# Lower priority for the additions of the shared products, and new scheduler clocks for the FFN, in a one-core hybrid layer

## The chip, the cores and the metric

The kernel runs on one core of a Trainium2 chip, in one launch. The metric is device microseconds of that core, median over runs. Of the core's engines, TensorE (PE) does the matrix products, VectorE (DVE) and ScalarE (ACT) do the elementwise work, and SyncE (SP) issues almost all of the DMAs.

## The reference

One layer on 256 rows of width 2048, all in float32: RMS norm, one wide input projection, three mixers (mLSTM, attention with forget gates, a conformer convolution), an output projection with a residual, and an FFN. The change touches the FFN alone, which is over half of the time:

```python
x = x + jnp.concatenate([y_m, y_a, y_c], axis=-1) @ w_out
h2 = rmsnorm(x, norm_ffn)
x = x + jnp.square(jax.nn.relu(h2 @ w_up)) @ w_down     # w_up 2048x8192, w_down 8192x2048
...
return rmsnorm(x, final_norm)
```

## The kernel before

**Splits.** To keep float32 accuracy, every operand of a big product is split into a rounded part `hi` and a remainder `lo`, and three products (hi·hi, hi·lo, lo·hi) are accumulated. The weights are split on the fly. One DMA brings a *unit* of 1 MB (4 chunks of 128 rows x 512 columns) into a tile `raw`, of which there are four (`NRAW`). A unit is used in two *steps* of two chunks each. For a step ACT writes `hi` (L424, or L396 in the steps described below), DVE writes `lo` = `raw` - `hi` (L443, or L399), and PE then does the step's matmuls (L57). There are five `hi` and five `lo` tiles (`NHL`), given out in the order in which the instructions are issued; a tile is free again when PE has finished the step that used it. The splits of a step are put up when PE has finished the step five earlier.

**The FFN** goes over the hidden width in four quarters, q = 0 to 3. In a quarter, four blocks of `w_up` make `hid` (16 steps and more of plain matmuls); then two *pairs* of column blocks of `w_down` (p = 0 and p = 1, each 2 x 512 columns) are multiplied, four row groups per pair. A plain step of `w_down` is 12 matmuls of 128x512. In row group 1 of a pair the 2x2 block product is done with seven products instead of eight: seven steps of 6 matmuls, in the order p3, p1, p2, p5, p7, p6, p4 (`SEVEN`). p5, p7, p6 and p4 multiply differences of weight pieces; DVE makes each difference in place in the `raw` tile (L383, "the sum" below) before it is split. In q = 3 the second pair is plain. So there are seven such blocks of seven steps.

**The shared products.** p1, p5, p6 and p7 go to PSUM banks of their own (`extra`). `add_up` collects them: in q = 0 ACT copies them into `acc` (first pair) or into a tile named `fnb` (second pair), in q = 1 to 3 DVE adds them to it (L1218). After the last quarter of a pair (q = 3 for the first, q = 2 for the second) four steps `g` of two DVE instructions each combine the four collected products and add them to the residual `x2t` (L1232 to L1245).

**The order** on ACT, DVE, PE and SP is made when the program is built, by a list scheduler with a clock per engine. Each task has an engine, a cost in us, predecessors and a priority (lower goes first). For each engine `best` takes, among the tasks that are ready at the engine's clock, the one with the lowest priority, then the oldest. PE's clock is advanced by a fixed time per step. The result is one fixed sequence per engine; on the chip an engine takes its sequence strictly in that order and waits where an operand isn't there. A split has priority -1, an addition of a shared product -2 and a step `g` -1.5, so both go ahead of splits that are ready at the same time.

Of the kernel before, what the change touches and what calls it, by code (L numbers as in the profile page):

```python
# [6 lines left out]
F32 = mybir.dt.float32  # L7
# [26 lines left out]
def trunk(ctx: ExitStack, tc, x, norm_mix, w_in, b_in, mlstm_conv_w, mlstm_conv_b,  # L34
# [3 lines left out]
    x, w_in, w_out, w_up, w_down, out = x[0], w_in[0], w_out[0], w_up[0], w_down[0], out[0]  # L38
# [15 lines left out]
    act, dve, pe, pool_e = nc.scalar, nc.vector, nc.tensor, nc.gpsimd  # L54
# [5 lines left out]
    clock = dict(act=0.0, dve=0.0, pool=0.0, pe=0.0, ctl=0.0)  # L60
# [32 lines left out]
    def t_act(cost, fn, *a, **kw):  # L93
        return task("act", cost, fn, *a, **kw)

    def t_dve(cost, fn, *a, **kw):
        return task("dve", cost, fn, *a, **kw)
# [87 lines left out]
    def ca(n, ps=False):  # L185
        return 0.11 + 0.00083 * n + (0.05 if ps else 0.0)

    def cd(n):
        return 0.13 + 0.00105 * n
# [47 lines left out]
    for name, lst in rows.items():  # L237
        rowp[name] = sbt(pl("early"), [P, P], "row" + name)
        colt[name] = sbt(base, [P, P], "col" + name)
        r = 0  # L240
# [80 lines left out]
    hl = {}  # L321
# [3 lines left out]
    loaded = {}  # L325
# [28 lines left out]
    halves = {}  # L354
# [5 lines left out]
    steps = []  # L360
    sums = {}
# [9 lines left out]
    def piece(u, h):  # L371
        return raws[u][0][:, 2 * h:2 * h + 2, :]

    def sum_task(i):

        s = steps[i]
        e, p = s["e"], s["p"]
        o, l, r = {"p5": ((e, 0), (e - 1, 0), (e, 0)),
                   "p7": ((e - 1, 0), (e - 1, 1), (e - 1, 0)),
                   "p6": ((e - 1, 1), (e - 1, 1), (e, 0)),  # L380
                   "p4": ((e, 1), (e, 1), (e - 1, 1))}[p]
        after = [halves[i - {"p5": 2, "p7": 3, "p6": 5, "p4": 4}[p]]] + [sums[k] for k in (i - 1, i - 2) if k in sums]
        sums[i] = t_dve(cd(1024), lambda: dve.tensor_sub(piece(*o), piece(*l), piece(*r)),  # L383
                        after + [loaded[e - 1], loaded[e]], prio=-1)
        return sums[i]

    def split_seven(i, deps):
        s = steps[i]
        u, h = s["u"], s["h"]
        if s["p"] in ("p5", "p7", "p6", "p4"):  # L390
            deps = deps + [sum_task(i)]

        def hi():
            t = sbt(base, [P, 2, 512], "hi", F32R, bufs=NHL)
            hl[i] = [t, sbt(base, [P, 2, 512], "lo", F32R, bufs=NHL)]
            act.activation(t, piece(u, h), AF.Copy)  # L396

        a = his[i] = t_act(ca(1024), hi, deps + [loaded.setdefault(u, Task("none", 0.0, None)), his[i - 1]], prio=-1)
        halves[i] = t_dve(cd(1024), lambda: dve.tensor_sub(hl[i][1], piece(u, h), hl[i][0].bitcast(F32)),  # L399
                          [a], prio=-1)  # L400
        if s["p"] == "p4":
            e = s["e"]
            f1 = [sums[i], halves[i - 1], halves[i - 2]]
            f2 = [halves[i], halves[i - 3]]
            c = t_ctl(lambda: load(e - 1 + NRAW, max(t.fin for t in f1)), f1)
            t_ctl(lambda: load(e + NRAW, max(t.fin for t in f2)), f2 + [c])

    his = {}

    def split_tasks(i, deps):  # L410

        if i >= len(steps):
            return
        if steps[i]["p"]:
            split_seven(i, deps)
            return
        u, h = steps[i]["u"], steps[i]["h"]
        d = units[u]
        n = len(d["ks"]) // 2

        def hi():
            t = sbt(base, [P, n, d["w"]], "hi", F32R, bufs=NHL)
            hl[i] = [t, sbt(base, [P, n, d["w"]], "lo", F32R, bufs=NHL)]
            act.activation(t, raws[u][0][:, h * n:(h + 1) * n, :], AF.Copy)  # L424

        deps = deps + [loaded.setdefault(u, Task("none", 0.0, None))]
        prio = -1 if i >= NHL else -2.005 + 0.02 * i
        a = his[i] = t_act(ca(1024), hi, deps + [his.get(i - 1)], prio=prio)
        last = [a]
        if d["g"]:  # L430
            c, m = (2 * NH, 0) if d["gside"] == "left" else (NF, 2 * NH)
            o = 0 if d["gside"] == "left" else d["w"]
            kr = slice(d["ks"][h * n], d["ks"][h * n] + n)
            wh, wl = wg[:, kr, m:m + c], wg[:, kr, NG + m:NG + m + c]
            ga = t_act(ca(n * c), lambda: act.activation(wh, raws[u][1][:, h * n:(h + 1) * n, o:o + c], AF.Copy),
                       deps, prio=-0.5)
            gd = t_dve(cd(n * c), lambda: dve.tensor_sub(wl, raws[u][1][:, h * n:(h + 1) * n, o:o + c],
                                                         wh.bitcast(F32)), [ga], prio=-0.5)
            gate_parts.append(gd)
            last.append(gd)  # L440

        def lo():
            dve.tensor_sub(hl[i][1], raws[u][0][:, h * n:(h + 1) * n, :], hl[i][0].bitcast(F32))  # L443

        b = t_dve(cd(1024), lo, [a], prio=prio)
        halves[i] = b
        if h == 1:
            if d["g"]:
                last.append(halves[i - 1])
            frees = [b, halves[i - 1]] + last + gate_parts  # L450
            t_ctl(lambda: load(u + NRAW, max(t.fin for t in frees)), frees)
# [109 lines left out]
    for j in range(2):  # L561
        d = []
        stats.append(d)
        for h in range(4):
            a = xs_stat[j][:, h:h + 1]
# [8 lines left out]
    for j in range(2):  # L574
# [9 lines left out]
        for h in range(4):  # L584
            o = xt[j][:, cut(h)]
            if h % 2:
                scaled[j, h] = t_act(0.6, lambda o=o, rs=rs: act.activation(o, o, AF.Copy, scale=rs), [d] + stats[1],
                                     prio=-2.9 + 0.2 * h)
            else:
                scaled[j, h] = t_dve(0.45, lambda o=o, rs=rs: dve.tensor_scalar(o, o, rs, None, op0=OP.mult), [d] + stats[1],  # L590
                                     prio=-2.9 + 0.2 * h)
# [9 lines left out]
    for c2 in range(KC // 2):  # L601
        b = mx_buf()
        ts = []
# [146 lines left out]
    for j in range(2):  # L750
        b = mx_buf()
# [454 lines left out]
    def add_up(p, q, o, fin):  # L1206

        ts = []
        for m, x in enumerate(("p1", "p5", "p6", "p7")):
            def f(m=m, x=x):  # L1210
                if (p, 0) not in acc:
                    acc[p, 0] = sbt(pl("late"), [P, 4, 512], "acc0") if p == 0 else \
                        sbt(pl("late"), [P, D], "fnb").rearrange("p (m n) -> p m n", m=4)
                t = acc[p, 0][:, m, :]
                if q == 0:
                    act.activation(t, o["extra"][x].t, AF.Copy)
                else:
                    dve.tensor_add(t, t, o["extra"][x].t)  # L1218

            deps = [o["done"][x], late_open] + ts[-1:]  # L1220
            if q == 0:
                ts.append(t_act(ca(512, True), f, deps, prio=-2, uses=[o["extra"][x]]))
            else:
                ts.append(t_dve(cd(512), f, deps, prio=-2, uses=[o["extra"][x]]))
        if not fin:
            return []

        def g(i):
            a1, a5, a6, a7 = (acc[p, 0][:, m, :] for m in range(4))

            def out(j, c, t):
                dve.scalar_tensor_tensor(x2[0][:, j, cut(c)], t, rs2[:, j:j + 1], x2[0][:, j, cut(c)],  # L1232
                                         op0=OP.mult, op1=OP.add)

            if i == 0:
                dve.tensor_add(a6, a6, a1)
                out(0, 2 * p, a1)
            elif i == 1:
                dve.tensor_add(a7, a7, a6)
                out(1, 2 * p, a7)  # L1240
            elif i == 2:
                dve.tensor_add(a6, a6, a5)
                out(0, 2 * p + 1, a6)
            else:
                dve.tensor_add(a5, a5, a7)  # L1245
                out(1, 2 * p + 1, a5)

        gs = [ts[-1]]
        for i in range(4):
            gs.append(t_dve(2 * cd(512), lambda i=i: g(i), [gs[-1], rs_t], prio=-1.5))  # L1250
        return gs[1:]

    def x2_ap(j, sl):
# [116 lines left out]

    NU = len(units)
    NS = len(steps)
    items = [(i, (0, 1)) for i in range(NS - 4)]
    for j in range(2):
        items += [(i, (j,)) for i in range(NS - 4, NS)]
# [7 lines left out]
    for i, toks in items:  # L1383
        u, half = steps[i]["u"], steps[i]["h"]
        d = units[u]
        if steps[i]["p"]:
            p, o = steps[i]["p"], steps[i]["o"]
            new = [o["extra"][p]] if p in o["extra"] else []
            need = [halves[i], chunk["sums%d" % o["q"]]] + [chunk[d["b"].key, k % KC] for k in d["ks"]]
            force(lambda: all(t.fin is not None for t in need) and room(new) is not None)  # L1390
            start = max([clock["pe"], room(new)] + [t.fin + LAT for t in need])
            take(new)
            for x_ in new:
                x_.t = bank(o["tag"])
            seven_matmuls(i)
            clock["pe"] = start + 1.3
            if new:
                o["done"][p].fin = clock["pe"]
            split_tasks(i + NHL, [done_at(clock["pe"])])
            extras()  # L1400
            continue
# [22 lines left out]
        if "force_log" in globals():  # L1424
            globals()["force_log"].append((i, clock["pe"], start))
        matmuls(i, toks)
        clock["pe"] = start + (2.6 if len(toks) == 2 else 1.3)
        if d["last"] and half == 1:
            for f in (toks if b.kind == "A" else range(b.n)):
                b.done[f].fin = clock["pe"]  # L1430
# [37 lines left out]
```

## Time and profile before

| | |
|---|---|
| median of 3 runs | 1162.3 us (1162.22, 1162.30, 1165.46) |
| profiled execution: its time, its span | 1167.01 us, 1164.9 us |
| mean granted clock of PE over the span | 0.988 |
| PE, DVE, ACT busy | 1135.5, 804.3, 602.3 us |
| share of PE in the chain that ended last | 95% |

The profile is one execution; the span runs from its first to its last instruction, and the time adds what lies around it (2.1 us). A granted clock of 1.00 is 2.4 GHz, 0.50 is 1.2 GHz; a value between is a stretch that has both. Matmuls overlap in the trace, so PE's pace is read from the starts of two rows.

### The profile page before, as it was taken

What the parts mean: (1) busy time and instruction counts of PE and PEld (TensorE: products, weight loads), DVE (VectorE), ACT (ScalarE), POOL (GpSimd) and SP (SyncE); (2) the same over time, 40 slices, a digit from 0 to 9 for tenths busy, and PEclk for the clock granted to TensorE, in tenths of its full rate; (3) what the DMA queues carried; (4) which work ended last, traced back from release to release, by engine and by line L of the source; (5) the groups of instructions that cost most, each with busy time, mean ns of one, the idle gap of its engine ahead of it and who ended that gap; (6) DMA issues with size and microseconds to landing.
All of it is one profiled execution on the core that took longest, in us unless ns stands there. A gap on an engine that the chain in (4) does not pass through costs nothing.

```text
span 1164.9 us, 14898 instructions
## 1 busy us (share of the span) xinstructions
PE 1135.5 (97%) x5838; PEld 962.3 (83%) x5838; DVE 804.3 (69%) x1083; ACT 602.3 (52%) x840; POOL 17.6 (2%) x40
## 2 busy tenths in 40 slices
PE   8999999999999999999999999999999989999796
PEld 6888888888888888888888887888887878888585
DVE  6679988886665565668765668675658685667663
ACT  6454366777775454445444454444445343544353
POOL 1000000000000000000000000000000000000000
PEclk8999999999999999999999999999999999999899
DMA  8756654557555555555485554476563666653642
GB/s 299 239 181 190 203 155 145 171 155 235 164 179 182 181 181 181 181 187 184 139 285 181 181 187 156 164 253 185 164 216 127 212 224 209 181 181 109 217 145 73
DMA packets 127694, 214.93 MB, mean 185 GB/s; under 512 B 3676, under 2 KB 44936, under 8 KB 127240
## 3 DMA queue, kind: packets, MB, share of 16 engines
q1 hardware_dynamic: 127016, 212.92, 56.3%
q10 hardware_dynamic: 608, 1.06, 0.3%
q8 instruction: 46, 0.75, 0.3%
q14 instruction: 24, 0.20, 0.0%
HBM read 211.87 MB, written 2.10 MB: 184 GB/s over the span
## 4 chain that ended last, share of the span: by engine, by line
PE 95%; DVE 2%; DMA 1%; issue 1%; ACT 0%; POOL 0%; POOLq 0%; ACTq 0%; DVEq 0%
PE mm L57 65%; PE mx L57 29%; DMA x<-in_x_dram 1%; DVE lo L399 0%; DVE x2t L1232 0%; DVE lo L443 0%; PE mx L1162 0%; DMA rowp<-in_norm_mix_dram 0%; DVE acc L1218 0%; PE mx L925 0%; POOL st L294 0%; PE mx L610 0%; ACT x2t L1362 0%; PE mx L958 0%; DVE fnb L1218 0%
## 5 line engine op out<-in xcount | busy, mean ns | idle before, releaser
L443 DVE TENSOR_TENSOR lo<-raw,hi 128x1024 fp32r<-128x1024 f32 x364 | 442.5, 1224 | 288.4 <-ACT hi L424 287.0
L424 ACT ACTIVATE hi<-raw 128x1024 fp32r<-128x1024 f32 x364 | 384.2, 1061 | 426.9 <-PE mm L57 282.1
L57 PE MATMUL mm<-x,hi 128*128 128x512 f32 x640 | 227.8, 400 | 0.0
L57 PE MATMUL mm<-h,hi 128*128 128x512 f32 x512 | 181.5, 399 | 0.0
L57 PE MATMUL mx<-h,hi 128*128 128x512 f32 x512 | 181.2, 399 | 0.0
L57 PE MATMUL mm<-x,lo 128*128 128x256 f32 x640 | 179.5, 280 | 0.0
L57 PE MATMUL mm<-hi,hid 128*128 128x512 f32 x556 | 174.6, 391 | 0.4 <-ACT hi L396 0.4
L57 PEld LDWEIGHTS mm<-x,hi 128*128 128x128 f32 x640 | 120.2, 188 | 28.8 <-ACT tmp L522 0.4
L57 PE MATMUL mm<-h,lo 128*128 128x256 f32 x512 | 143.8, 281 | 0.0
L57 PE MATMUL mx<-h,lo 128*128 128x256 f32 x512 | 143.8, 281 | 0.0
L57 PEld LDWEIGHTS mm<-hi,hid 128*128 128x128 f32 x556 | 105.2, 189 | 22.7 <-ACT hi L396 0.8
L57 PEld LDWEIGHTS mm<-x,lo 128*128 128x128 f32 x640 | 120.9, 189 | 0.1
L57 PEld LDWEIGHTS mm<-h,hi 128*128 128x128 f32 x512 | 96.2, 188 | 24.0 <-DVE x2t L1150 0.2
L57 PEld LDWEIGHTS mx<-h,hi 128*128 128x128 f32 x512 | 96.2, 188 | 23.9
L57 PE MATMUL mm<-lo,hid 128*128 128x512 f32 x278 | 109.3, 393 | 5.4 <-DVE lo L443 3.8
L57 PE MATMUL mx<-hi,hid 128*128 128x512 f32 x328 | 106.0, 399 | 0.7 <-ACT hi L396 0.7
L57 PEld LDWEIGHTS mm<-h,lo 128*128 128x128 f32 x512 | 96.7, 189 | 0.1
L57 PEld LDWEIGHTS mx<-h,lo 128*128 128x128 f32 x512 | 96.7, 189 | 0.1
L396 ACT ACTIVATE hi<-raw 128x1024 fp32r<-128x1024 f32 x49 | 52.1, 1064 | 66.2 <-DVE raw L383 27.0
L57 PE MATMUL mm<-hi,y 128*128 128x512 f32 x256 | 80.4, 392 | 0.0
L57 PEld LDWEIGHTS mx<-hi,hid 128*128 128x128 f32 x328 | 63.4, 193 | 15.2 <-ACT hi L396 1.6
L57 PE MATMUL mx<-lo,hid 128*128 128x512 f32 x164 | 65.8, 401 | 8.7 <-DVE lo L399 8.7
(224 smaller groups left out, 1154.3 us busy)
## 6 DMA issues: line engine op xcount, KB each, us to landing
raw<-in_w_up_dram SPq DMA_DIRECT2D x64, 1024.0 KB, 5.4
raw<-in_w_down_dram SPq DMA_DIRECT2D x64, 1024.0 KB, 5.2
raw<-in_w_in_dram SPq DMA_DIRECT2D x45, 1024.0 KB, 5.3
raw<-in_w_out_dram SPq DMA_DIRECT2D x16, 1024.0 KB, 5.1
raw<-in_w_in_dram SPq DMA_DIRECT2D x4, 1032.0 KB, 5.1
raw<-in_w_in_dram SPq DMA_DIRECT2D x2, 1088.0 KB
x<-in_x_dram SPq DMA_DIRECT2D x8, 256.0 KB, 6.1
x2t<-in_x_dram SPq DMA_DIRECT2D x2, 1024.0 KB
```

The lines of the kernel that those rows point to most:

```text
L57: pe.matmul(o, l, r, start=start, stop=stop, skip_group_check=True)
L396: act.activation(t, piece(u, h), AF.Copy)
L424: act.activation(t, raws[u][0][:, h * n:(h + 1) * n, :], AF.Copy)
L443: dve.tensor_sub(hl[i][1], raws[u][0][:, h * n:(h + 1) * n, :], hl[i][0].bitcast(F32))
```

## The change

Four things, all in the program that makes the order; no instruction is added or removed on any engine.

- The additions (L1218) and ACT's copies go from priority -2 to -0.6, the steps `g` from -1.5 to -0.5: behind the splits (-1) instead of ahead of them.
- The costs of the FFN's splits are set to 1.06 (`hi`) and 1.22 (`lo` and the sum), where the old formulas gave 0.96 and 1.205.
- PE's clock goes on by 1.36 us for each half of a `w_down` step (2.72 a step, before 2.6) and for each of the seven (before 1.3), and by 2.82 for a `w_up` step (before 2.6).
- The `hi` of a plain step no longer has the `hi` of the step before as its predecessor, unless that step is one of the seven.

```diff
-        a = his[i] = t_act(ca(1024), hi, deps + [loaded.setdefault(u, Task("none", 0.0, None)), his[i - 1]], prio=-1)
-        halves[i] = t_dve(cd(1024), lambda: dve.tensor_sub(hl[i][1], piece(u, h), hl[i][0].bitcast(F32)),
+        a = his[i] = t_act(C_HI, hi, deps + [loaded.setdefault(u, Task("none", 0.0, None)), his[i - 1]], prio=-1)
+        halves[i] = t_dve(C_LO, lambda: dve.tensor_sub(hl[i][1], piece(u, h), hl[i][0].bitcast(F32)),
...
+    C_HI, C_LO = 1.06, 1.22
...
-        a = his[i] = t_act(ca(1024), hi, deps + [his.get(i - 1)], prio=prio)
+        late_ = i >= 2 * U_FFN
+        a = his[i] = t_act(C_HI if late_ else ca(1024), hi, deps + [his.get(i - 1) if i and steps[i - 1]["p"] else None], prio=prio)
...
-                ts.append(t_act(ca(512, True), f, deps, prio=-2, uses=[o["extra"][x]]))
+                ts.append(t_act(ca(512, True), f, deps, prio=-0.6, uses=[o["extra"][x]]))
             else:
-                ts.append(t_dve(cd(512), f, deps, prio=-2, uses=[o["extra"][x]]))
+                ts.append(t_dve(cd(512), f, deps, prio=-0.6, uses=[o["extra"][x]]))
...
-            gs.append(t_dve(2 * cd(512), lambda i=i: g(i), [gs[-1], rs_t], prio=-1.5))
+            gs.append(t_dve(2 * cd(512), lambda i=i: g(i), [gs[-1], rs_t], prio=-0.5))
...
-            clock["pe"] = start + 1.3
+            clock["pe"] = start + 1.36
...
-        clock["pe"] = start + (2.6 if len(toks) == 2 else 1.3)
+        clock["pe"] = start + (1.36 * len(toks) if i >= FFN_STEP and b.kind == "A" else 2.82 if i >= FFN_STEP else 2.6 if len(toks) == 2 else 1.3)
```

Up to the FFN the sequences of all engines are the same as before, and PE's is the same throughout. Three places show what moves. A name's number is that of its buffer; it differs between the two programs for the same data. Lines in the changed kernel are 2 higher (L1220 is L1218).

Place one is DVE in q = 3, first pair, at the seven steps. Before, the additions of p1 and p5 stand just ahead of these rows, each before a sum or split that was ready; then come the sum for p4, the additions of p6 and p7, the four steps `g`, and the split of p4:

```order
L383 TENSOR_TENSOR raw_8826<-raw_8826,raw_8787 128x1024
L1218 TENSOR_TENSOR acc0_4918<-acc0_4918,mm_9028 128x512
L1218 TENSOR_TENSOR acc0_4918<-acc0_4918,mm_9019 128x512
L1236 TENSOR_TENSOR acc0_4918<-acc0_4918 128x512
L1232 SCALAR_TENSOR_TENSOR x2t_2582<-acc0_4918,st_99,x2t_2582 128x512
L1239 TENSOR_TENSOR acc0_4918<-acc0_4918 128x512
L1232 SCALAR_TENSOR_TENSOR x2t_2582<-acc0_4918,st_99,x2t_2582 128x512
L1242 TENSOR_TENSOR acc0_4918<-acc0_4918 128x512
L1232 SCALAR_TENSOR_TENSOR x2t_2582<-acc0_4918,st_99,x2t_2582 128x512
L1245 TENSOR_TENSOR acc0_4918<-acc0_4918 128x512
L1232 SCALAR_TENSOR_TENSOR x2t_2582<-acc0_4918,st_99,x2t_2582 128x512
L399 TENSOR_TENSOR lo_9036<-raw_8826,hi_9035 128x1024
```

Now, from the split of p6 on:

```order
L399 TENSOR_TENSOR lo_9001<-raw_8787,hi_9000 128x1024
L383 TENSOR_TENSOR raw_8810<-raw_8810,raw_8787 128x1024
L1220 TENSOR_TENSOR acc0_4918<-acc0_4918,mm_8993 128x512
L1220 TENSOR_TENSOR acc0_4918<-acc0_4918,mm_9011 128x512
L445 TENSOR_TENSOR lo_9027<-raw_8852,hi_9026 128x1024
L399 TENSOR_TENSOR lo_9033<-raw_8810,hi_9032 128x1024
L445 TENSOR_TENSOR lo_9045<-raw_8852,hi_9044 128x1024
L445 TENSOR_TENSOR lo_9055<-raw_8894,hi_9054 128x1024
L445 TENSOR_TENSOR lo_9059<-raw_8894,hi_9058 128x1024
L445 TENSOR_TENSOR lo_9079<-raw_9030,hi_9078 128x1024
L1220 TENSOR_TENSOR acc0_4918<-acc0_4918,mm_9036 128x512
L1220 TENSOR_TENSOR acc0_4918<-acc0_4918,mm_9019 128x512
```

The split of p4 is now `lo_9033`; ahead of it, behind the sum, stand the additions of p1 and p5 and one split (`lo_9027`), and the additions of p6, p7 and the steps `g` come five and more splits later. The first pairs of q = 1 and q = 2 read the same, there without the steps `g`.

Place two is DVE in q = 2, second pair, behind the seven steps. Before, the split of the first plain step (`lo_7952`) is followed by the additions of p6 and p7, the steps `g` and only then the split of the second plain step (`lo_7965`):

```order
L443 TENSOR_TENSOR lo_7952<-raw_7813,hi_7951 128x1024
L1218 TENSOR_TENSOR fnb_5218<-fnb_5218,mx_7968 128x512
L1218 TENSOR_TENSOR fnb_5218<-fnb_5218,mx_7954 128x512
L1236 TENSOR_TENSOR fnb_5218<-fnb_5218 128x512
L1232 SCALAR_TENSOR_TENSOR x2t_2582<-fnb_5218,st_99,x2t_2582 128x512
L1239 TENSOR_TENSOR fnb_5218<-fnb_5218 128x512
L1232 SCALAR_TENSOR_TENSOR x2t_2582<-fnb_5218,st_99,x2t_2582 128x512
L1242 TENSOR_TENSOR fnb_5218<-fnb_5218 128x512
L1232 SCALAR_TENSOR_TENSOR x2t_2582<-fnb_5218,st_99,x2t_2582 128x512
L1245 TENSOR_TENSOR fnb_5218<-fnb_5218 128x512
L1232 SCALAR_TENSOR_TENSOR x2t_2582<-fnb_5218,st_99,x2t_2582 128x512
L443 TENSOR_TENSOR lo_7965<-raw_7813,hi_7964 128x1024
```

Now, from the split of p4 on:

```order
L399 TENSOR_TENSOR lo_7941<-raw_7779,hi_7940 128x1024
L445 TENSOR_TENSOR lo_7951<-raw_7813,hi_7950 128x1024
L445 TENSOR_TENSOR lo_7965<-raw_7813,hi_7964 128x1024
L445 TENSOR_TENSOR lo_7978<-raw_7851,hi_7977 128x1024
L445 TENSOR_TENSOR lo_7988<-raw_7851,hi_7987 128x1024
L445 TENSOR_TENSOR lo_8006<-raw_7954,hi_8005 128x1024
L1220 TENSOR_TENSOR fnb_5218<-fnb_5218,mx_7943 128x512
L445 TENSOR_TENSOR lo_8025<-raw_7954,hi_8024 128x1024
L1220 TENSOR_TENSOR fnb_5218<-fnb_5218,mx_7967 128x512
L1220 TENSOR_TENSOR fnb_5218<-fnb_5218,mx_7956 128x512
L1238 TENSOR_TENSOR fnb_5218<-fnb_5218 128x512
L1234 SCALAR_TENSOR_TENSOR x2t_2582<-fnb_5218,st_99,x2t_2582 128x512
```

Five splits now stand ahead of the second addition, and a split stands between any two steps `g`.

Place three is ACT in q = 3, first pair, at the seven steps. Before, after p7, p6 and p4 the splits go on in the order of the steps:

```order
L396 ACTIVATE hi_8989<-raw_8787 128x1024
L396 ACTIVATE hi_9000<-raw_8787 128x1024
L396 ACTIVATE hi_9035<-raw_8826 128x1024
L424 ACTIVATE hi_9042<-raw_8868 128x1024
L424 ACTIVATE hi_9047<-raw_8868 128x1024
L424 ACTIVATE hi_9052<-raw_8908 128x1024
```

Now:

```order
L396 ACTIVATE hi_8989<-raw_8787 128x1024
L396 ACTIVATE hi_9000<-raw_8787 128x1024
L425 ACTIVATE hi_9026<-raw_8852 128x1024
L396 ACTIVATE hi_9032<-raw_8810 128x1024
L425 ACTIVATE hi_9044<-raw_8852 128x1024
L425 ACTIVATE hi_9054<-raw_8894 128x1024
```

`hi_9026`, the `hi` of the second plain step after the seven, goes ahead of p4's (`hi_9032`) and of the first plain step's (`hi_9044`). So it is the one that gets p1's `hi` and `lo` tiles, and DVE's `lo_9027` in place one is its `lo`. This turn is made at the first pair of every quarter.

Two more things move: in each quarter a split of `w_up` changes place with the `lo` of a piece of `hid`, and on SP the DMA of `final_norm` goes behind four loads of `raw`.

## Rows read from the trace of the kernel before

**Rows 1.** The page, part 1: busy us (share of the span) xinstructions.
```profile
PE 1135.5 (97%) x5838; PEld 962.3 (83%) x5838; DVE 804.3 (69%) x1083; ACT 602.3 (52%) x840; POOL 17.6 (2%) x40
```
**Rows 2.** Waits of PE: who for whom, us in total, times, longest us.
```profile
PE mx L57 <- DVE lo L399: 8.7, 2, 7.1
PE mm L57 <- DVE lo L443: 3.8, 1, 3.8
```
**Rows 3.** Timeline of PE, q = 3 first pair: start, duration, instruction, [idle before <-releaser].
```profile
1074.31 0.39 PE L57 MATMUL mm<-hi,xsums 128*128 128x512 f32 x1
...
1078.16 0.39 PE L57 MATMUL mm<-hi,xsums 128*128 128x512 f32 x1
...
1086.50 0.79 PE L57 MATMUL mx<-lo,hid 128*128 128x512 f32 x1 [7.07 <-DVE lo L399]
...
1092.45 0.39 PE L57 MATMUL mx<-lo,hid 128*128 128x512 f32 x1
```
**Rows 4.** Timeline of PE, q = 1 first pair.
```profile
716.15 0.39 PE L57 MATMUL mm<-hi,xsums 128*128 128x512 f32 x1
...
719.06 0.50 PE L57 MATMUL mx<-lo,hid 128*128 128x512 f32 x1 [1.64 <-DVE lo L399]
...
723.01 0.65 PE L57 MATMUL mx<-hi,hid 128*128 128x512 f32 x2
```
**Rows 5.** Timeline of PE, q = 2 first pair.
```profile
895.12 0.39 PE L57 MATMUL mx<-hi,xsums 128*128 128x512 f32 x1
...
898.02 0.50 PE L57 MATMUL mm<-lo,hid 128*128 128x512 f32 x1 [1.64 <-DVE lo L399]
...
899.72 0.61 PE L57 MATMUL mm<-hi,hid 128*128 128x512 f32 x2
```
**Rows 6.** Timeline of PE, q = 2 second pair.
```profile
943.92 0.61 PE L57 MATMUL mm<-hi,hid 128*128 128x512 f32 x2
948.33 0.79 PE L57 MATMUL mm<-lo,hid 128*128 128x512 f32 x1 [3.79 <-DVE lo L443]
...
952.31 0.62 PE L57 MATMUL mm<-hi,hid 128*128 128x512 f32 x2
```
**Rows 7.** Stretches: us, busy (x) of PE, PEld, DVE, ACT, POOL, PEclk, DMA, GB/s.
```profile
719.00:723.00 4.00, 3.94 (x10) 3.11 (x11) 4.00 (x5) 2.71 (x3) 0.00 (x0) 0.58 0.97 333
895.00:903.00 8.00, 5.99 (x26) 4.42 (x25) 7.46 (x8) 6.50 (x7) 0.00 (x0) 1.00 0.88 294
1079.00:1091.50 12.50, 5.43 (x13) 4.05 (x14) 12.39 (x16) 4.72 (x5) 0.00 (x0) 0.60 0.53 185
```
**Rows 8.** Timeline of DVE, q = 3 first pair.
```profile
1070.88 2.35 DVE L399 TENSOR_TENSOR lo<-raw,hi 128x1024 fp32r<-128x1024 f32 x2
...
1073.75 1.22 DVE L399 TENSOR_TENSOR lo<-raw,hi 128x1024 fp32r<-128x1024 f32 x1
1075.87 0.69 DVE L1218 TENSOR_TENSOR acc<-acc,mm 128x512 f32<-128x512 f32 x1 [0.90 <-PE mm L57]
1076.47 1.22 DVE L383 TENSOR_TENSOR raw<-raw 128x1024 f32<-128x1024 f32 x1
1078.59 1.28 DVE L1218 TENSOR_TENSOR acc<-acc,mm 128x512 f32<-128x512 f32 x2 [0.90 <-PE mm L57]
...
1085.22 1.22 DVE L399 TENSOR_TENSOR lo<-raw,hi 128x1024 fp32r<-128x1024 f32 x1
```
**Rows 9.** Timeline of ACT, q = 3 first pair.
```profile
1071.84 1.06 ACT L396 ACTIVATE hi<-raw 128x1024 fp32r<-128x1024 f32 x1 [0.34 <-PE mx L57]
...
1078.78 3.88 ACT L424 ACTIVATE hi<-raw 128x1024 fp32r<-128x1024 f32 x4
```
**Rows 10.** Timeline of DVE, q = 2 second pair.
```profile
934.40 1.22 DVE L383 TENSOR_TENSOR raw<-raw 128x1024 f32<-128x1024 f32 x1
935.53 0.68 DVE L1218 TENSOR_TENSOR fnb<-fnb,mx 128x512 f32<-128x512 f32 x1
...
947.06 5.76 DVE L443 TENSOR_TENSOR lo<-raw,hi 128x1024 fp32r<-128x1024 f32 x5
```

More of the change, by code (lines that the diff above doesn't have):

```diff
@@ L382, in sum_task @@
         after = [halves[i - {"p5": 2, "p7": 3, "p6": 5, "p4": 4}[p]]] + [sums[k] for k in (i - 1, i - 2) if k in sums]
-        sums[i] = t_dve(cd(1024), lambda: dve.tensor_sub(piece(*o), piece(*l), piece(*r)),
+        sums[i] = t_dve(C_LO, lambda: dve.tensor_sub(piece(*o), piece(*l), piece(*r)),
                         after + [loaded[e - 1], loaded[e]], prio=-1)
@@ L443, in lo @@
             dve.tensor_sub(hl[i][1], raws[u][0][:, h * n:(h + 1) * n, :], hl[i][0].bitcast(F32))
-        b = t_dve(cd(1024), lo, [a], prio=prio)
+        b = t_dve(C_LO if late_ else cd(1024), lo, [a], prio=prio)
         halves[i] = b
@@ L1372, in trunk @@
     NS = len(steps)
+    FFN_STEP = 2 * U_FFN
     items = [(i, (0, 1)) for i in range(NS - 4)]
```

## The prediction

> **What bounds the kernel now.** I read the busy times first [rows 1]: PE is busy for 97% of the span, DVE for 69%, ACT for 52%. PE sets the time, and what an edit to DVE's and ACT's order can give back is PE's lost time only. So the second view is the list of PE's waits [rows 2]. Nearly all of the waiting in the FFN is for one kind of instruction, a `lo` that DVE writes: 8.7 us on the steps p4 (L399), 3.8 us on a plain step (L443). The reader should see that the waits are few and long, so they have places. The third view is PE's timeline at the places. There are four: A (q = 1, first pair), B (q = 2, first pair), C (q = 2, second pair), D (q = 3, first pair).
>
> PE's undisturbed pace comes from D: 17 starts lie between 1074.31 and 1078.16 [rows 3], so 3.85 / 17 = 0.2265 us per 512-column matmul. With it, the loss at a place is the time between two starts less the matmuls issued between them.
> - A [rows 4]: 716.15 to 723.01 is 6.86 us for 12 matmuls (2.72): 4.14 lost.
> - B [rows 5]: 895.12 to 899.72 is 4.60 us for 9 (2.04): 2.56 lost.
> - C [rows 6]: 943.92 to 952.31 is 8.39 us for 12 (2.72): 5.67 lost.
> - D [rows 3]: 1078.16 to 1092.45 is 14.29 us for 17 (3.85): 10.44 lost.
>
> Together 22.8 us. The loss has two parts. The pause itself, up to the first `lo` matmul less two matmuls' pace (0.45), is 719.06 - 716.15 - 0.45 = 2.46 at A, 2.45 at B, 3.96 at C and 7.89 at D, 16.8 us in all. The other 6.0 us are clock: after the pauses at A and D the granted clock is 0.58 and 0.60 for a while, a mix of the 2.4 GHz level and the 1.2 GHz level, but at B it stays 1.00 after the same pause [rows 7]. So the clock's share (A 1.7, B 0.1, C 1.7, D 2.5) isn't fixed by the pause alone.
>
> The fourth view is DVE at D [rows 8]. After the sum for p4 (1076.47) it waits 0.90 us for PE, does the additions of p6 and p7, then the four steps `g`, and starts the split of p4 only at 1085.22. PE needed that `lo` at 1078.16 + 0.45 = 1078.61. ACT isn't the cause: it had made p4's `hi` and the four next ones by 1078.78 + 3.88 = 1082.66 [rows 9]. The additions stand in front of a ready split. At C likewise five ready splits start only at 947.06 [rows 10].
>
> **The change part by part.** No instruction is added or taken away, so DVE's total work stays; what counts is what stands in front of the split that PE needs next.
>
> *Additions and `g` behind splits.* I walk DVE's new row at D (place one) with the spacings of rows. Two splits in a row take 2.35, so one 1.22 long is followed after 1.14 [rows 8]; a sum is followed after 1.13 [rows 10] and an addition after 0.60 (1075.87 to 1076.47) [rows 8]. Nothing ahead of 1070.88 moves. Splits of p5 and p7 start at 1070.88 and 1072.02. p6 starts at 1073.16 (its `hi` is ready at 1071.84 + 1.06 = 1072.90 [rows 9]), instead of 1073.75. The sum for p4 starts at 1074.30, the addition of p1 at 1075.43, that of p5 at 1076.03. PE has p5 ready: before, the same addition was released at 1075.87. Then `lo_9027` at 1076.63, and the split of p4 at 1077.77. Its `hi` is ready at 1074.30 + 1.22 + 1.06 = 1076.58. It ends at 1079.00, and PE starts 0.06 later (as 1085.22 + 1.22 is followed by 1086.50), at 1079.06. PE wants it at 1078.61. **So 0.45 us of the pause stays at D, because two additions and a split of a later step still stand ahead of p4's.** A and B have the same row and PE pattern, so I take 0.45 there too. At the first pair of q = 0 the additions are ACT's; without two of them the split of p4 comes 0.60 x 2 earlier, and there is nothing to lose.
>
> The bounds of this remainder: nothing, if the adds slip in anywhere earlier; with all eight instructions at full length (six of 1.22, two of 0.69) the chain is 8.7 instead of 8.1 us, so 1.05 us. I take 0.45, since the spacings are measured in the same stretch. Does so short a pause lower the clock? The nearest row is B, where five times as much did not; I take no.
>
> At C (place two) the splits of the plain steps start right behind p4's, about 938.4, not up to 947.06 [rows 10]. PE uses a plain step in 12 x 0.2265 = 2.72 us, DVE splits one in 1.14; with one step `g` in between (1.4 us at most, two instructions of about 0.7) it is 2.5, still under 2.72. The first such gap has two additions as well (3.7 us), and DVE is by then several steps ahead. I count all of C as gone. The same goes for the steps `g` at D.
>
> *Clocks and costs.* They act by the order alone. The `w_up` turns put one `lo` of `hid` 1.14 us later; it is read a good two blocks of `w_up` later, which is the cover. The DMA of `final_norm` goes behind four loads on SP; its first reader comes after the next quarter's first pair. Loads of `raw` wait for the splits of the seven, which come earlier at A, B and D. All these I cost at nothing.
>
> **Sum.** 22.8 - 3 x 0.45 = 21.4 us off the profiled execution: 1167.0 becomes 1145.6, the span 1143.5. The median before is 1162.3, 4.7 us under that execution. If the difference is the profiler's, 1162.3 - 21.4 = 1140.9. If it is clock that those runs didn't lose (4.7 of the 6.0), only 16.8 - 1.35 = 15.4 is sure and the time is up to 1146.9. The three runs differ by 3.2 us among themselves, about two such shares of clock, so I lean to the later end of the middle: **1144 us**.
>
> **The rivals.**
> - *Pauses stay at the first pairs.* By place one the split of p4 still has company. With the 1.05 us of the bound and a clock share of 1.7 each, A, B and D keep 3 x 2.75 = 8.2 us: 1162.3 less 22.8 - 8.2 = 14.6 is 1147.7; if the runs before had only lost the pauses and 1.3 of clock, 18.1 - 8.2 = 9.9 and the time is 1152.4. For it: the walk does find the `lo` late. Against it: B.
> - *No change*, because something else stands right behind the additions: `hi`, or a load. Then 1162. Against it: at 1085.22 five splits ran without a wait between them at C and ACT was done 2.5 us before [rows 9, 10].
> - *Slower, through the tiles.* At each first pair the second plain step takes p1's tiles (place three). The split of the fifth plain step therefore gets the second one's tiles, and can't begin until PE is 2 steps past p4, 5.44 us; `hi` and `lo` take 2.3; PE comes to it after 4 steps, 10.87. That leaves 3.1 us. DVE and ACT stand in line behind it meanwhile. It decides when that split is held up further: beyond 3.1 us PE pauses, and at 3.1 + 21.4 / 4 = 8.5 us at all four first pairs the gain is gone; 10 us late would give 4 x 6.9 - 21.4 = 6 us more than before, 1168. I see no row that would hold it so long.
> - *Banks held too long.* The additions of p6 and p7 at D now wait behind that fifth split, 5.44 + 2.3 after p4, and end about 9 us after it. Their banks are next wanted 8 plain steps after p4, 21.7 us. Past that PE waits; 1 us over at each of five places would make it 1149. The row for it: DVE waits 0.90 us for PE before an addition (1075.87), while the sum behind it was ready [rows 8]. So a waiting instruction holds up all behind it.
>
> The Trainium skill, in "PSUM — Partial Sum Buffer", section "Engine vs sequencer instructions", says that VectorE's and ScalarE's queues are strictly first in, first out. The 0.90 us agrees. By that rule the late additions can't slip past a split that waits, which speaks against putting them last; it makes the last two rivals possible, and by the rows the margins (12 us and 3.1 us) cover it.
>
> **How the numbers follow.** The forecast (1138.5 to 1148) has 0.78; pauses at the first pairs (1147 to 1153) 0.13; banks 0.03; no change 0.03; slower 0.03. The range 1138.5 to 1151 runs from the case of 1140.9 with the remainders gone as well and a little clock, to the middle of the second case; it leaves out less than 2 in 10. A measurement of this kernel can tell about 0.3%, 3.5 us, from no change. Faster 0.94, same 0.03, slower 0.03.
>
> **What would show it.** In the changed kernel's profile PE's waits for `lo` L401 (before L399) should fall from two long ones of 8.7 us together [rows 2] (and B's) to some 0.5 us at each of the three first pairs, that for L445 (before L443) should be gone, and no half clock should follow them. Adds of p6 and p7 and `g` should stand between splits, DVE idle less before p4 and more later. Wrong would be: pauses of 1 us and more at p4 with a clock under 1.00 behind them; a new wait of PE for an addition (banks) or for the `hi` of the fifth plain step; or the same 22 us at other places.

## The result and the profile after

The changed kernel takes 1143.39 us (median of 4 runs, 1142.24 to 1143.96), the kernel before 1163.78 us beside it (4 runs, 1162.22 to 1165.46): ratio 0.9823, 95% interval 0.9803 to 0.9844. Forecast were 1144 us and faster; both held. The profiled execution after took 1142.24 us, its span is 1140.2 us and its mean granted clock 0.997.

The first view is the page of the changed kernel, the busy times of the engines:

```profile
PE 1125.3 (99%) x5838; PEld 957.7 (84%) x5838; DVE 802.9 (70%) x1083; ACT 601.9 (53%) x840; POOL 17.6 (2%) x40
```

Against [rows 1], DVE and ACT do the same work (within 1.4 us), while PE is busy for 10.2 us less with the same 5838 matmuls: before, some of them ran at a lowered clock, and some of q = 0 a little slower at full clock (see "The sum" below). The second view is the list of PE's waits after, all of it (who for whom, us in total, times, longest):

```profile
PE mx L612 <- DVE x L592: 3.4, 1, 3.4
PE mm L552 <- POOL gb L272: 1.4, 1, 1.4
PE mx L57 <- DVE lo L399: 0.5, 2, 0.2
PE mm L57 <- DVE lo L399: 0.2, 1, 0.2
```

The two long waits of [rows 2] are gone. Three short ones for p4's `lo` are left, which the profile prints as 0.25 us each in the timeline; the first two rows belong to the start of the program, outside the FFN. The third view is the table of stretches around A, B, C and D after (us, busy and count of PE, PEld, DVE, ACT, POOL, then PEclk, DMA share, GB/s):

```profile
700.00:730.00 30.00, 29.75 (x132) 24.33 (x131) 23.91 (x24) 15.30 (x15) 0.00 (x0) 1.00 0.60 210
880.00:905.00 25.00, 24.75 (x110) 20.19 (x109) 19.46 (x19) 13.48 (x13) 0.00 (x0) 1.00 0.71 248
925.00:960.00 35.00, 35.00 (x163) 29.23 (x162) 30.55 (x34) 16.38 (x17) 0.00 (x0) 1.00 0.79 270
1045.00:1095.00 50.00, 49.75 (x219) 40.86 (x219) 46.09 (x50) 26.83 (x32) 0.00 (x0) 1.00 0.57 195
```

At C (the third row) PE is busy for all of the 35.00 us; in the others only the 0.25 us are missing. PEclk is 1.00 in all four; behind the pauses at A and D it had been 0.58 and 0.60 [rows 7]. The fourth view is PE's timeline at D after:

```profile
1063.43 0.39 PE L57 MATMUL mm<-hi,xsums 128*128 128x512 f32 x1
1063.65 0.39 PE L57 MATMUL mx<-hi,hid 128*128 128x512 f32 x1
1064.29 0.50 PE L57 MATMUL mx<-lo,hid 128*128 128x512 f32 x1 [0.25 <-DVE lo L399]
1064.62 0.62 PE L57 MATMUL mx<-hi,hid 128*128 128x512 f32 x2
```

By the prediction's measure the pause is 1064.29 - 1063.43 - 0.45 = 0.41 us (before 7.89 [rows 3]). Up to the next start, 1064.62, 1.19 us go by for three matmuls (0.68), so 0.51 us are lost in all. A and B have the same three distances. The fifth view is DVE at D after, the answer to [rows 8]:

```profile
1056.14 3.49 DVE L399 TENSOR_TENSOR lo<-raw,hi 128x1024 fp32r<-128x1024 f32 x3
1059.55 1.22 DVE L383 TENSOR_TENSOR raw<-raw 128x1024 f32<-128x1024 f32 x1
1060.68 1.28 DVE L1220 TENSOR_TENSOR acc<-acc,mm 128x512 f32<-128x512 f32 x2
1061.88 1.22 DVE L445 TENSOR_TENSOR lo<-raw,hi 128x1024 fp32r<-128x1024 f32 x1
1063.02 1.22 DVE L399 TENSOR_TENSOR lo<-raw,hi 128x1024 fp32r<-128x1024 f32 x1
1064.15 4.62 DVE L445 TENSOR_TENSOR lo<-raw,hi 128x1024 fp32r<-128x1024 f32 x4
1068.69 1.28 DVE L1220 TENSOR_TENSOR acc<-acc,mm 128x512 f32<-128x512 f32 x2
1069.89 1.22 DVE L445 TENSOR_TENSOR lo<-raw,hi 128x1024 fp32r<-128x1024 f32 x1
1071.02 0.69 DVE L1238 TENSOR_TENSOR acc<-acc 128x512 f32<-128x512 f32 x1
```

The reader should see that no row carries an idle time in brackets: p5, p7, p6, the sum, two additions, the split of a later step (L445), p4 at 1063.02, four more splits, and only then the additions of p6 and p7 and the steps `g`. Nothing that waits for PE stands ahead of p4 any more.

### The profile page after: what moved, and what is told of

Read it like the earlier page. It is cut to its first block, busy times and chain, and to the rows that moved or that the text cites. A ratio compares the mean times of both kernels' runs of the same rounds, so it can differ in the third digit from the quotient of the medians.

```text
span 1140.2 us, 14902 instructions
## 1 busy us (share of the span) xinstructions
PE 1125.3 (99%) x5838; PEld 957.7 (84%) x5838; DVE 802.9 (70%) x1083; ACT 601.9 (53%) x840; POOL 17.6 (2%) x40
## 3 DMA queue, kind: packets, MB, share of 16 engines
q10 hardware_dynamic: 608, 1.06, 0.3%
## 4 chain that ended last, share of the span: by engine, by line
PE 94%; DVE 4%; ACT 1%; DMA 1%; issue 1%; SPq 0%; POOL 0%; POOLq 0%; ACTq 0%; DVEq 0%
PE mm L57 65%; PE mx L57 28%; DVE lo L399 2%; DVE raw L383 1%; DMA x<-in_x_dram 1%; DVE lo L445 0%; PE mx L1164 0%; DVE acc L1220 0%; ACT hi L396 0%; SPq L255 0%; PE mx L927 0%; POOL st L294 0%; PE mx L612 0%; ACT x2t L1364 0%; PE mx L960 0%
## 5 line engine op out<-in xcount | busy, mean ns | idle before, releaser
L445 DVE TENSOR_TENSOR lo<-raw,hi 128x1024 fp32r<-128x1024 f32 x364 | 443.4, 1224 | 278.4 <-ACT hi L425 276.6
L57 PE MATMUL mx<-hi,hid 128*128 128x512 f32 x328 | 103.1, 390 | 0.0
L399 DVE TENSOR_TENSOR lo<-raw,hi 128x1024 fp32r<-128x1024 f32 x49 | 59.2, 1222 | 12.0 <-ACT hi L396 11.9
```

What stands on the lines that cost most here:

```text
L57: pe.matmul(o, l, r, start=start, stop=stop, skip_group_check=True)
L399: halves[i] = t_dve(C_LO, lambda: dve.tensor_sub(hl[i][1], piece(u, h), hl[i][0].bitcast(F32)), [a], prio=-1)
```

## The experiments

Theory: an addition or a step `g` that stands ahead of a ready split is the whole loss, so the priorities do all of it. Rivals: the new clocks and costs do it; the steps `g` matter as much as the additions; late additions cost something elsewhere (tiles, banks). Runs of one group were made beside the same runs of the kernel before: 1164.18 us for the first four experiments, 1164.12 for the next four, 1162.69 for the last four.

**Priorities alone** (the kernel before with both edits of priority):

```diff
-  ts.append(t_act(ca(512, True), f, deps, prio=-2, uses=[o["extra"][x]]))
+  ts.append(t_act(ca(512, True), f, deps, prio=-0.6, uses=[o["extra"][x]]))
...
-  ts.append(t_dve(cd(512), f, deps, prio=-2, uses=[o["extra"][x]]))
+  ts.append(t_dve(cd(512), f, deps, prio=-0.6, uses=[o["extra"][x]]))
...
-  gs.append(t_dve(2 * cd(512), lambda i=i: g(i), [gs[-1], rs_t], prio=-1.5))
+  gs.append(t_dve(2 * cd(512), lambda i=i: g(i), [gs[-1], rs_t], prio=-0.5))
```

> The kernel before with the priorities alone (additions -0.6, steps g -0.5); costs, clocks and predecessors as before. Order: the split of p4 stands right behind the additions of p1 and p5 at the first pairs, without a split of a later step between. Theory (what cost the time is the additions and g in front of splits, and the priority alone takes them away): by the walk the lo of p4 then ends 1.14 us earlier than in the changed kernel, 0.7 us before PE wants it, so no pause at A, B, C or D: about 1142 us, as fast as the changed kernel or up to 1.4 us faster. Rival (the corrected clocks are needed, since with the old ones the scheduler believes PE to be faster than it is): pauses of 2 us and more stay at some places, 1150 us or more.

1142.51 us, ratio 0.9811 (0.9793 to 0.9828). PE's list of waits, of this kernel and complete, has no `lo` at all:

```profile
PE mx L610 <- DVE x L590: 3.4, 1, 3.4
PE mm L550 <- POOL gb L272: 1.4, 1, 1.4
```

So the priorities alone give the whole gain, and the remainder at A, B and D isn't theirs.

**Clocks and costs alone** (the changed kernel with the old priorities and the old predecessor):

> The changed kernel with the old priorities (-2, -1.5) and the old predecessor; only costs and clocks are new. Order: at the first pairs the split of p4 now comes before the additions of p6 and p7 (and at D before g), but at D the split of the first plain step still stands behind additions and g, and C is as before. Theory (position in DVE's sequence decides, whatever put it there): A and B lose nothing, C keeps 5.7 us, D waits about 6.5 us at the first plain step plus some 2.5 us of clock, so 14.7 of the 22.8 us stay: about 1155.7 us (1153 to 1158). Rival (only the priority matters): as before, 1163.8 us.

1159.86 us, ratio 0.9961 (0.9947 to 0.9974): about 4 of the 20 us, and 1.9 us over the upper end of what was expected. The waits of this kernel for the `lo` of a plain step:

```profile
PE mx L57 <- DVE lo L445: 7.0, 2, 6.2
PE mm L57 <- DVE lo L445: 5.0, 3, 3.8
```

The pauses have mostly moved from p4 to the plain step behind it: 6.24 us at D and 3.79 at C, and 0.81 each at A and B, which the expectation had not counted. DVE at A in this kernel shows them:

```profile
712.50 1.23 DVE L399 TENSOR_TENSOR lo<-raw,hi 128x1024 fp32r<-128x1024 f32 x1 [0.61 <-ACT hi L396]
713.77 1.28 DVE L1220 TENSOR_TENSOR acc<-acc,mm 128x512 f32<-128x512 f32 x2
714.98 6.89 DVE L445 TENSOR_TENSOR lo<-raw,hi 128x1024 fp32r<-128x1024 f32 x6
```

The clocks let p4's split past two additions, but not the six splits behind it. The profiled execution took 1158.73 us, 3.0 over the expected time; the two uncounted pauses are 1.6 of that (2 x 0.81). The rest, and why the other runs were up to 2.6 us later, is not traced.

**Predecessor alone** (the kernel before, one line):

```diff
-  a = his[i] = t_act(ca(1024), hi, deps + [his.get(i - 1)], prio=prio)
+  a = his[i] = t_act(ca(1024), hi, deps + [his.get(i - 1) if i and steps[i - 1]["p"] else None], prio=prio)
```

> The kernel before with the predecessor dropped alone. Order: at the first pairs of q = 1 to 3 one split of a later step now also stands in front of the split of p4, filling time in which DVE waited 0.9 us for PE. Theory (it gives nothing): pauses at A, B and D 0 to 0.3 us longer, C the same: 1163 to 1166 us, same as before. Rival (the free hi is a part of the gain): faster by 3 us or more.

1165.6 us, ratio 1.0014 (1.0001 to 1.0028). It gives nothing, and if anything costs 1.4 us. The waits for p4's `lo` are 0.15 us longer at each of A, B and D (1.79, 1.79 and 7.22), and a new one of 0.95 stands at the first pair of q = 0, which the expectation had not counted.

**The changed kernel with the old predecessor** (the same line, turned round):

> The changed kernel with the old predecessor put back. Order: at the first pairs no split stands in front of the split of p4 any more, else as the changed kernel. Theory (the remainder of 0.4 us at A, B and D comes from that one split): no wait of PE for a lo in the FFN at all, about 1142 us, 1.3 us under the changed kernel, which the time alone hardly tells. Rival (dropping the predecessor is needed for the gain): 1147 us or more, with pauses at the first pairs.

1142.4 us, ratio 0.9812 (0.9795 to 0.9829), and no wait of PE for a `lo` in the FFN. So the dropped predecessor, which lets the split of a plain step go ahead of p4's, makes the remainder of 0.41 us.

**Steps `g` early again** (the changed kernel with `g` at -1.5):

> The changed kernel with the steps g back at -1.5; additions at -0.6. Order: the four steps g stand in one block of 5.5 us again, but five (C) or six (D) splits further back than before. Theory (a block that long hurts only where the splits are not yet ahead of PE; a tile comes free for the next split as PE frees it, as the changed kernel's trace has it at D): no pause at C and D beyond the 0.4 us, 1143.4 us as the changed kernel. Rival (the prediction's tile rule, by which the fifth split waits until PE is two plain steps past p4): the split of the sixth plain step comes 2 us late at D, with 0 to 2 us of clock: 1145.5 to 1148 us.

1142.74 us, ratio 0.981 (0.9793 to 0.9826): as the changed kernel, and PE's list of waits has the same three short ones for p4's `lo` and no other in the FFN. The rival's late sixth split doesn't happen.

**Additions early again** (the changed kernel with the additions at -2). In the kernel that ran the predecessor is dropped as in the changed kernel; where the expectation speaks of the old one, it is wrong on that.

> The changed kernel with the additions back at -2 and the old predecessor; steps g at -0.5, costs and clocks new. Order: at the first pairs the split of p4 stands before the additions of p6 and p7, the split of the first plain step behind them. Theory (position decides): as in the kernel with new clocks alone, PE waits about 1 us at the first plain step at A, B and D, nothing at C, no clock: 1143.4 - 1.3 + 3 = 1145.1 us (1144 to 1147). Rival (the additions' priority is the main part of the gain): 1152 us or more.

1150.64 us, ratio 0.9879 (0.9862 to 0.9897), 3.6 us over the theory's upper end and 1.4 under the rival's bound. The order was not the expected one either: with the predecessor dropped, the additions of p6 and p7 stand ahead of p4's split, not behind it. DVE at D in this kernel:

```profile
1062.85 2.35 DVE L399 TENSOR_TENSOR lo<-raw,hi 128x1024 fp32r<-128x1024 f32 x2
1065.12 0.69 DVE L1220 TENSOR_TENSOR acc<-acc,mm 128x512 f32<-128x512 f32 x1
1065.72 1.22 DVE L399 TENSOR_TENSOR lo<-raw,hi 128x1024 fp32r<-128x1024 f32 x1
1066.86 1.22 DVE L383 TENSOR_TENSOR raw<-raw 128x1024 f32<-128x1024 f32 x1
1067.99 0.68 DVE L1220 TENSOR_TENSOR acc<-acc,mm 128x512 f32<-128x512 f32 x1
1068.59 1.22 DVE L445 TENSOR_TENSOR lo<-raw,hi 128x1024 fp32r<-128x1024 f32 x1
1070.56 1.29 DVE L1220 TENSOR_TENSOR acc<-acc,mm 128x512 f32<-128x512 f32 x2 [0.75 <-PE mm L57]
1071.76 1.22 DVE L399 TENSOR_TENSOR lo<-raw,hi 128x1024 fp32r<-128x1024 f32 x1
```

p4's split starts 8.91 us after p5's, in the changed kernel 6.88. The difference is the 0.75 us that DVE waits for PE in front of the additions of p6 and p7, their two spacings (1.20), and 0.08 of rounding. PE pauses 2.29 us each at A, B and D instead of 0.25. Those are 3 x 2.04 = 6.1 us; the clock adds up to (1 - 0.89) x 15 = 1.65 at A, by the stretches of this kernel from A, B and D on:

```profile
715.00:730.00 15.00, 13.32 (x52) 10.83 (x53) 9.61 (x9) 4.98 (x5) 0.00 (x0) 0.89 0.84 311
890.00:905.00 15.00, 12.71 (x56) 10.20 (x56) 11.85 (x12) 7.08 (x7) 0.00 (x0) 1.00 0.76 269
1070.00:1085.00 15.00, 12.71 (x57) 10.20 (x56) 14.37 (x17) 6.35 (x7) 0.00 (x0) 1.00 0.90 328
```

Together 7.8, against 1150.64 - 1143.39 = 7.25 measured. What stands ahead of a split costs its length and also what it waits for itself.

**Steps `g` late alone** (the kernel before, the `g` line of the first diff only):

> The kernel before with the steps g at -0.5 alone. Order: the additions stand where they stood, the steps g between splits. Theory (of the 16.8 us of pauses, the block g makes all of C and all of D but 2.5 us): pauses of 2.5 us stay at A, B and D, each with 0 to 1.7 us of clock: 1149.5 to 1154.6 us, about 1152. Rival (g is a small part, the additions the main one): 1158 us or more.

1151.0 us, ratio 0.988 (0.9862 to 0.9897), as expected. C is gone; A, B and D keep 0.37 us for `hi` and 1.64 for `lo` each.

**The late split made longer** (the changed kernel, DVE writes p4's `lo` four times; the values are the same):

```diff
-  halves[i] = t_dve(C_LO, lambda: dve.tensor_sub(hl[i][1], piece(u, h), hl[i][0].bitcast(F32)),
-                    [a], prio=-1)
+  def lo():
+      for _ in range(4 if s["p"] == "p4" else 1):
+          dve.tensor_sub(hl[i][1], piece(u, h), hl[i][0].bitcast(F32))
+  halves[i] = t_dve(C_LO, lo, [a], prio=-1)
```

> The changed kernel in which DVE writes the lo of p4 four times instead of once, the same values each time, at all seven blocks of seven steps; the scheduler's costs are left, so the order is the changed kernel's. The split is 3.4 to 3.7 us later. Theory (a late split of p4 costs PE its lateness, one for one, less what it was early, and then some clock): pauses of about 3.9 us at A, B and D, 2.9 at the first pair of q = 0, 1.7 at the three second pairs, 18.4 us more than the changed kernel, and 0 to 1.7 us of clock at each: 1162 to 1173 us. Rival (five tiles ahead cushion a late split, so that the pauses before had another cause): under 1150 us.

1173.38 us, ratio 1.0067 (1.0046 to 1.0087), 0.4 us over the upper end. PE at the first pair of q = 0, and at D, in this kernel (where p4's `lo` is written in L401):

```profile
543.31 0.79 PE L57 MATMUL mm<-lo,hid 128*128 128x512 f32 x1 [3.00 <-DVE lo L401]
...
1093.36 0.79 PE L57 MATMUL mx<-lo,hid 128*128 128x512 f32 x1 [4.03 <-DVE lo L401]
```

The four splits of p4 take 5.00 us in DVE's timeline there, so three of them add 5.00 - 1.22 = 3.78. At D PE waits 4.03 = 0.25 + 3.78: each part goes to PE one to one. By the prediction's measure the pause at q = 0 is 543.31 - 539.69 - 0.45 = 3.17 us (539.69 is the start of the second matmul before it), so that place had 3.78 - 3.17 = 0.61 us to spare. The clock cost more than the 1.7 us a place that were allowed for: it is 0.77 over the 15 us behind three of the four long pauses, up to 3.45 us each.

**Additions late alone** (the kernel before, the first two edits of the first diff, `g` left at -1.5):

> The kernel before with the additions of the shared products alone at priority -0.6; the steps g keep -1.5, the clocks and the predecessor are the old ones. Theory (the additions do all of it, and the steps g come late by themselves because each waits for an addition): 1142.5 us (1141.5 to 1144), no pause of PE for a split in the FFN. Rival (the steps g must also stand behind splits): at q = 3, first pair, the four steps g stand in one block of about 5.3 us ahead of plain splits that PE comes to, PE waits there for 1 us or more, with a lowered clock behind it: 1145 to 1149 us.

1141.89 us, ratio 0.9817 (0.9804 to 0.9831): two lines give the whole gain. DVE at D in this kernel:

```profile
1061.20 1.22 DVE L399 TENSOR_TENSOR lo<-raw,hi 128x1024 fp32r<-128x1024 f32 x1
1062.34 7.13 DVE L443 TENSOR_TENSOR lo<-raw,hi 128x1024 fp32r<-128x1024 f32 x6
1069.39 0.68 DVE L1218 TENSOR_TENSOR acc<-acc,mm 128x512 f32<-128x512 f32 x1
...
1072.71 0.68 DVE L1236 TENSOR_TENSOR acc<-acc 128x512 f32<-128x512 f32 x1
...
1077.47 0.75 DVE L1232 SCALAR_TENSOR_TENSOR x2t<-acc,st,x2t 128x512 f32<-128x512 f32 x1
1078.14 2.35 DVE L443 TENSOR_TENSOR lo<-raw,hi 128x1024 fp32r<-128x1024 f32 x2
```

Here the four steps `g` do stand in one block, 1072.71 to 1078.14. PE doesn't pause, because six splits of plain steps (from 1062.34) were made ahead of it. The first `g` has the last addition as its predecessor, so the four come late by themselves once the additions do. That is why `g` late alone gives 13.1 us (1164.12 to 1151.0), the larger part of the loss, and yet the edit to `g` adds nothing to that of the additions.

**Side by side**, the changed kernel, the same with the old predecessor, and the kernel before with both priorities:

> The changed kernel again, beside the two variants that leave the predecessor alone. Theory (the split that the dropped predecessor lets slip in ahead of p4's is the whole difference, 0.4 us at each of three places): 1143.4 us, 1.2 us above them. Rival (the difference seen so far is scatter): within 0.4 us of them.

> The changed kernel with the old predecessor of a step's hi put back. Theory: 1142.3 us, 1.2 us below the changed kernel. Rival: within 0.4 us of it.

> The kernel before with the additions at -0.6 and the steps g at -0.5 and nothing else. Theory: 1142.4 us, the same as the changed kernel with the old predecessor, so that the new clocks and costs are worth nothing once the priorities are in. Rival (the clocks are worth something): 0.5 us or more above it.

| kernel | us, range | ratio to before, interval |
|---|---|---|
| changed kernel | 1143.69, 1142.38 to 1143.92 | 0.983, 0.9817 to 0.9843 |
| changed kernel, old predecessor | 1142.22, 1140.79 to 1142.56 | 0.9818, 0.9804 to 0.9831 |
| before with both priorities | 1141.31, 1140.93 to 1142.67 | 0.9814, 0.9801 to 0.9827 |

The changed kernel is 1.5 us above the one with the old predecessor, but the intervals overlap, so the times only lean that way. PE's own time in the FFN says more: from the start of the first matmul on `h` to the start of the last on `hid`, it leaves out what varies ahead of the FFN. The changed kernel with the old predecessor:

```profile
430.09 0.39 PE L57 MATMUL mm<-h,hi 128*128 128x512 f32 x1
...
1129.98 0.39 PE L57 MATMUL mm<-hi,hid 128*128 128x512 f32 x1
```

The kernel before with both priorities:

```profile
431.06 0.39 PE L57 MATMUL mm<-h,hi 128*128 128x512 f32 x1
...
1130.95 0.39 PE L57 MATMUL mm<-hi,hid 128*128 128x512 f32 x1
```

Both are 699.89 us, and so is the kernel with the additions late alone (429.39 to 1129.29): the clocks, the costs and the edit to `g` are worth nothing once the additions are late. The changed kernel needs 701.34 (430.97 to 1132.31), so the dropped predecessor costs it 1.45 us; the kernel before needed 724.40 (430.86 to 1155.26).

## Why the prediction was right

- **Place and cause.** PE's lost time sat at A to D, and additions stood ahead of ready splits. The priorities alone remove it; the clocks and costs alone move it to the next step; the predecessor alone does nothing. The prediction took the order as a whole and did not say which edit does what. Its part "Clocks and costs", priced at nothing, was priced rightly; the predecessor was not priced by itself, though the split of a later step that it lets in ahead of p4's is in the walk. The two rows of additions would have been enough.
- **The walk at D.** From the start of p5's split to p4's it has 6.89 us, measured 6.88; to PE's restart 8.18, measured 8.15. The remainder, 0.45 forecast at each of A, B and D, is 0.41. The spare at q = 0 that follows from it (2 x 0.60 - 0.45 = 0.75) is 0.61.
- **What it passed over.** "ACT isn't the cause" leaves out that at A, B and D PE had first waited 0.37 us for p4's `hi`; these waits are part of its 16.8 us. At D ACT made that `hi` at 1077.81, after waiting for DVE's `raw`, the sum, and the sum stood behind the waiting addition of p5 [rows 8]. So this part too goes with the additions: it stays with `g` late alone and is gone with the additions late.
- **C and the steps `g`.** All of C counted as gone: PE is busy without a gap there.
- **The clock.** Taken to stay up after a pause of 0.45: it does, 1.00 in all four stretches.
- **The sum.** 21.4 us were worked out; the medians differ by 20.4. That 1144 is only 0.6 us off is partly luck: it was chosen between two sums, 1140.9 and 1146.9, and their base of 1162.3 became 1163.78 with a fourth run. Between the profiled executions it is 24.8 (1167.01 to 1142.24), of which A to D by the same working are 22.8 - 3 x 0.51 = 21.3. Of the rest, 1.5 us lie ahead of the FFN: PEclk in the first 30 us is 0.89 before and 0.94 after, (0.94 - 0.89) x 30 = 1.5. Another 1.7 are in the `w_up` blocks of q = 0, where PE takes 91.42 us from its first matmul on `h` to its first on `hid` (430.86 to 522.28), and 89.75 after (429.38 to 519.13), at a PEclk of 1.00 in both. The kernel with the predecessor dropped alone has 89.75 too, so this belongs to that one execution and not to the order; why PE's pace was lower there stays open. The last 0.2 or so are a short wait for p4's `lo` at the first pair of q = 0, which the prediction's four places leave out.
- **Rival "pauses stay at the first pairs".** It did not come true here: the short waits that stay are 0.25 us each, without a lower clock. With the additions at -2 such pauses do stay, and cost 7.25 us; that this is near the rival's 8.2 is chance, since they are longer (2.29 us) and the clock fell at one of the three only.
- **Rival "slower, through the tiles".** Its premise was wrong. It has the split of the fifth plain step wait until PE is two steps past p4. ACT's row at D after:

```profile
1061.85 3.12 ACT L425 ACTIVATE hi<-raw 128x1024 fp32r<-128x1024 f32 x3
1065.95 1.06 ACT L425 ACTIVATE hi<-raw 128x1024 fp32r<-128x1024 f32 x1 [0.98 <-DMA raw<-in_w_down_dram]
```

  That fifth `hi` starts at 1065.95 and had waited for its weights, while PE ends the second plain step only at about 1063.65 + 0.51 + 6 x 0.2265 + 5.44 = 1070.96. So the tiles are not tied to the order of issue as the description of the kernel has it, and the margin was wider than the 3.1 us.
- **Rival "banks held too long".** The additions of p6 and p7 end at 1068.69 + 1.28 = 1069.97, some 4.5 us after PE's last matmul of p4 (1065.52 by the same working) instead of the 9 forecast, and PE waits for none of them. The Trainium skill's rule of strictly first-in, first-out queues ("PSUM — Partial Sum Buffer", section "Engine vs sequencer instructions"), which spoke against putting them last, holds in the runs where the additions are early: the 0.75 us that they wait is paid by p4's split behind them. In the changed kernel no late addition on DVE waits for PE.

## What to carry to other kernels

In a list schedule, work whose result is needed late (collecting, adding up) should rank behind work that the busiest engine needs next, above all if it waits for that engine itself: its own wait is paid by everything behind it in the queue. Find the few long pauses of the busy engine first, and count at each what stands ahead of the instruction that it waits for, with lengths and waits. Then give each edit a run of its own: here two changed numbers hold the whole gain, and one of the other edits took a little of it back.

## What the runs showed of the hardware

The same pause sometimes lowered the granted clock behind it and sometimes did not. With additions early, 2.29 us of waiting at A, B and D gave 0.89, 1.00 and 1.00 in the stretches above. With `g` late alone the waits were 0.37 and 1.64 us at each place, and the stretches of that kernel from A, B and D on show:

```profile
713.00:728.00 15.00, 12.99 (x49) 10.04 (x48) 10.75 (x11) 8.22 (x9) 0.00 (x0) 0.89 0.88 306
892.00:907.00 15.00, 12.99 (x56) 10.22 (x55) 11.37 (x12) 9.10 (x9) 0.00 (x0) 1.00 0.89 312
1069.00:1084.00 15.00, 12.99 (x50) 10.06 (x49) 12.78 (x14) 8.05 (x9) 0.00 (x0) 0.89 0.89 309
```

A and D fall, B does not. With p4's split four times as long, the clock is 0.77 from the 3.00 us pause on and 1.00 after two of 1.86; in stretches of that kernel from q = 0's first pair and from the second pairs of q = 1 and q = 2 on:

```profile
540.00:555.00 15.00, 12.00 (x41) 9.40 (x40) 9.89 (x9) 5.80 (x8) 0.00 (x0) 0.77 0.74 262
771.00:786.00 15.00, 13.16 (x58) 10.87 (x59) 12.72 (x13) 5.88 (x6) 0.00 (x0) 1.00 0.84 282
955.00:970.00 15.00, 13.61 (x60) 11.26 (x61) 14.93 (x18) 5.72 (x6) 0.00 (x0) 1.00 0.83 283
```

Behind its three pauses of 4.03 us it is 0.89 at A, 0.77 at B and 0.77 at D (15 us from 724, 907 and 1090 on). With the predecessor dropped alone, 0.37 and 1.79 us at A and at B gave 0.89 at both. What decides it between equal pauses was not tried and stays open. It may be one reason why kernels with such pauses spread more from run to run: in the first set the kernel before ran from 1162.25 us, at a mean granted clock of 0.991, to 1166.4, at 0.986 (16 runs), the one with both priorities from 1140.96 to 1142.88, at 0.996 and 0.995 (4 runs).
